# Five pairs of split-weight buffers, four raw buffers, and the layer norms' weight subtractions on VectorE

## The chip, the cores and the metric

The kernel runs on one core of a Trainium2 chip, in one launch. The metric is the device time of an execution in microseconds (us). Times of the kernel before are the median of three runs.

## The reference

The program computes two transformer blocks in float32 for one sequence of 256 tokens with 1024 features. The first block makes a modulation from a condition vector, mixes the tokens by attention, a state-space scan and a pooled branch, and passes them through 16 experts, of which each token uses two. The second block is two layers of feed-forward, token mix, feed-forward and per-layer gate, with a layer norm behind each:

```python
def second_block(x, p, ln_g, ln_b, ffn_w1, ffn_w3, ffn_w2, w_in, ...):
    a = DEEPNORM_ALPHA_2
    for i in range(DEPTH_2):
        x = _layer_norm(a * x + MACARON_W * _swiglu(x, ffn_w1[i, 0], ffn_w3[i, 0], ffn_w2[i, 0]), ln_g[i, 0], ln_b[i, 0])
        mix = token_mixing(x, w_in[i], ...)
        x = _layer_norm(a * x + mix, ln_g[i, 1], ln_b[i, 1])
        x = _layer_norm(a * x + MACARON_W * _swiglu(x, ffn_w1[i, 1], ffn_w3[i, 1], ffn_w2[i, 1]), ln_g[i, 2], ln_b[i, 2])
        ple = jax.nn.sigmoid(x @ ple_w_gate[i]) * (p[i] @ ple_w_proj[i])
        x = _layer_norm(a * x + ple, ln_g[i, 3], ln_b[i, 3])
    return x
```

The token mix has three branches: an RWKV recurrence, a gated delta rule (which inverts small triangular matrices) and a gated linear attention.

## The kernel before

Nearly all the time goes into products of the 256 tokens with weights that stream in from HBM. Each weight matrix is cut into chunks of 128 x 1024 values, 512 KB. A chunk (`chunk_ap`, L139 to L152) is loaded by SyncE's (SP's) queue into a buffer `raw`; ScalarE (ACT) casts it to `whi`, a rounded float32 that TensorE (PE) multiplies at its faster rate (L112); a subtraction raw - whi gives the rest, `wlo` (L113, which the profile shows under the helper's line L88). The activations are split in the same way into `xh` and `xl`, or `ffh` and `ffl`. PE makes three products for each block: whi with xh, whi with xl, wlo with xh, into PSUM banks `psA`, `psB`, `psC` (L85). There are five buffers `raw`, and three each of `whi` and `wlo`; a `raw` is free again when its subtraction is done, a `whi` and a `wlo` when PE has used them. The modulation's weights (`ada`, L260) pass through the same five `raw` buffers, but are multiplied and summed on VectorE (DVE) into `adacc` instead.

The subtraction runs on DVE, or on GpSimd (POOL) while the counter `s.on_pool` is above 0. The counter falls by one with each chunk and is set anew at certain places: at the start (L351), in the first mix (L370), at the end of `first_out` (L769), in `experts` (L922), at the end of `moe` (L981) and of `res_ln` (L1057), in the token mix (L1710, L1716), and ahead of the projection of the per-layer input (L1768).

A scheduler sets the order of the instructions on each engine by priorities and by when buffers come free: chunks are split 400 places ahead of the work in which they stand (`SPLIT_AHEAD`), and a layer norm goes ahead of other work by 2000 (`LN_AHEAD`). Each engine then runs its list strictly in order.

Between two stages stands a layer norm (`res_ln`, L1039, with `ln_apply`, L237). For each half of the tokens DVE adds the residual (`lnr<-psA,x`), takes the statistics (`lnst`, `lnmv`), and ACT the root (`lnrs`); DVE normalises in two halves of 512 columns (`lnr<-lnr,lnmv,lng` and `x<-lnr,lnrs,lnb`); PE transposes x into `psC` (L117), ACT and DVE split it into `xh` and `xl`. Ahead of the experts and behind them the same is written out in `first_out` (L706) and `moe` (L943, with the names `mo`). The gains and offsets `lng` and `lnb` are loaded by POOL's queue (`load_rows`, L703). The next stage's first products use the first half of the tokens while the second half is still being normalised.

```python
    def split(s, hi, lo, src, eng=None):
        s.nc.scalar.copy(hi, src)
        s.sub(lo, src, hi.bitcast(F32), eng)
```

Of the kernel before, what the change touches and what calls it, by code (L numbers as in the profile page):

```python
# [9 lines left out]
F32 = mybir.dt.float32  # L10
# [9 lines left out]
D = 1024  # L20
# [3 lines left out]
SSD_AHEAD = 100  # L24


# which tiles take turns in which slots (by lifetime), and how many slots there are
# [29 lines left out]
class Net:  # L57
# [13 lines left out]
    # ---- tiles  # L71
# [11 lines left out]
    # ---- engines  # L83
# [51 lines left out]
    # ---- dense products  # L135
# [3 lines left out]
    def chunk_ap(s, ap, nk, ncol):  # L139
        with s.tc.high_priority(SPLIT_AHEAD):  # L140
            raw = s.wp.tile([128, nk, ncol], F32, name="raw", bufs=5)
            hi = s.wp.tile([128, nk, ncol], F32R, name="whi", bufs=3)
            lo = s.wp.tile([128, nk, ncol], F32R, name="wlo", bufs=3)
            s.nc.sync.dma_start(raw, ap)
            s.split(hi, lo, raw, s.nc.gpsimd if s.on_pool > 0 else None)
# [27 lines left out]
    def cols_s(s, w, c0, x, nk=8):  # L173
        """[128, 2, 256] bank with columns c0..c0+256 of x @ w, features on partitions."""
# [5 lines left out]
    def cols_s_half(s, ps, w, cols, x, k):  # L180
        """the part of cols_s, for several blocks of columns, that takes features k*128 .. k*128+512."""
# [3 lines left out]
    def few_cols(s, w, x, out):  # L185
        """a few columns of x @ w, as rows of out [n, 256] and in a bank [128, 2, n] with tokens on partitions."""
# [13 lines left out]
    def cols_m(s, w, c0, ncol, x, *together):  # L200
        """two banks [128, ncol], tokens on partitions (K = 1024)."""
# [5 lines left out]
    def by_token(s, todo, x, *together):  # L207
        """so many chunks at a time (one in the end) do their products with the first half of the tokens before
        those with the second half."""
# [12 lines left out]
    def to_T(s, x, t, out, k0=0, n=8):  # L222
        """token block t ([128, n*128]) -> hi/lo parts with features on partitions."""
# [7 lines left out]
    # ---- layer norm over r [128, 1024] (in place scratch) -> out  # L231
    def warm(s, dep, f=AF.Sqrt):
        """has the function's table loaded once dep [128, 1] is there."""
        j = s.t([128, 1], "warm")
        s.act(j, dep, f, scale=0.0, bias=1.0)
# [23 lines left out]
    # ---- first block  # L259
    def ada(s, sections):  # L260
        """the modulation's sections as columns of s.mod; yields after every chunk of the weights."""
        nc, a = s.nc, s.a
        for i in sections:
            acc = s.t([128, 1024], "adacc")
            for k in range(8):
                raw = s.wp.tile([128, 1024], F32, name="raw", bufs=5)
# [13 lines left out]
    def ada_row(s, i, dst, **k):  # L280
        """section i as a row on every partition."""
# [7 lines left out]
    def start(s):  # L289
# [28 lines left out]
        # shift and scale, half of the features at a time  # L318
# [3 lines left out]
        def stream(h):  # L322
            acc = s.t([128, 2, 512], "adacc")
            for k in range(8):
                raw = s.wp.tile([128, 2, 512], F32, name="raw", bufs=5)
# [24 lines left out]
        for p, c in zip(first, s.first_cols):  # L350
            s.on_pool = 1  # L351
# [22 lines left out]
    def log1pexp(s, y, shape, tag):  # L374
        """y -> max(y, 0) + log1p(exp(-|y|)), in place; log1p(e) = ln(u) * e / (u - 1), u = 1 + e."""
# [21 lines left out]
    def forget(s, w, x):  # L397
        """softplus(-f) of the forget gates, softplus(dt), exp(a_log)."""
# [12 lines left out]
    def attention(s, w, x, first, qT, kT, v):  # L411
# [7 lines left out]
        for g in range(2):  # L419
# [5 lines left out]
            if g == 0:  # L425
                nlf, dt, al = s.forget(w, x)
                # negated cumulative forget gate, per key: rows [2 (hi, lo), head, key]
# [17 lines left out]
            # heads 8g + 2i + par; even and odd ones run side by side in the array's halves  # L445
# [55 lines left out]
    def ssd_in(s, w, x, dt, al):  # L501
# [29 lines left out]
        # decays  # L531
# [18 lines left out]
    def pool_zgate(s, w, x):  # L550
        """the pooled branch; and z * (1 + tanh(z / 2)) = 2 silu(z), tokens on partitions."""
# [9 lines left out]
        for g in range(4):  # L561
# [18 lines left out]
            # the mean over the window, which the first tokens do not fill, less the token itself  # L580
# [64 lines left out]
    def merge_gates(s, w, x):  # L645
        """m = (1 + tanh(g0/2)) y_att + (1 + tanh(g1/2)) y_pool; g2 kept: all twice the gate."""
# [15 lines left out]
    def ssd_out(s):  # L662
        nc, a = s.nc, s.a
        nw = s.mod[:, 48:64]
        # z holds 2 y: mean square over 512 of y is ss / 2048
# [28 lines left out]
        # merged (twice the gated sum), then w_out  # L694
# [11 lines left out]
    def first_out(s):  # L706
        """w_out, the two layer norms, and the router's input."""
# [19 lines left out]
        # the router's product with (n * sc + sh) as one with n, which sh's share precedes  # L727
# [41 lines left out]
        s.on_pool = 3  # L769
# [1020 lines left out]
```

## Time and profile before

| what | us |
|---|---|
| median of the runs shown | 2696.99 |
| all runs | 2691.86, 2696.99, 8709.61 |
| span of the profiled execution, first to last instruction | 2692.0 |
| its PE, DVE, ACT, POOL busy time | 2537.4, 1801.1, 1293.3, 286.6 |

The page gives no time of the profiled execution other than its span, which lies at the lowest of the runs. The run of 8709.61 was disturbed; the other two lie 0.2% apart. An engine's busy time is the sum of its instructions; where PE is busy all the time, nothing that another engine does less of shortens the span. The granted clock (PEclk) is the share of full speed that the throttle gave TensorE in a stretch: 1.00 is 2.4 GHz, and the lower level of 1.2 GHz is 0.5. A wait such as "PE psC L117 <- DVE x L106" is idle time of the first engine that ended when the second had done the named instruction. All times inside the program are us from the first instruction.

### The profile page before, as it was taken

How to read it: one execution, taken by the hardware profiler on the slowest of the kernel's cores; microseconds unless marked ns; L12 is line 12 of the kernel's file. 1: busy time of each engine (PE TensorE's matmuls, PEld its weight loads, DVE VectorE, ACT ScalarE, POOL GpSimd, SP SyncE). 2: the span in 40 equal slices, each digit the busy share in tenths (PEclk: the TensorE clock that was granted, in tenths of full speed). 3: DMA queues.
4: the chain of work that ended last, by engine and by line, in shares of the span. 5: the costliest groups of instructions: out<-in, count | busy, mean ns of one | idle time of the engine just before them, and what ended most of it. 6: DMA issues, size and time to landing. Idle time of an engine off the chain costs nothing.

```text
span 2692.0 us, 41847 instructions
## 1 busy us (share of the span) xinstructions
PE 2537.4 (94%) x16713; PEld 2279.5 (85%) x16713; DVE 1801.1 (67%) x2487; ACT 1293.3 (48%) x1737; POOL 286.6 (11%) x195
## 2 busy tenths in 40 slices
PE   6999999969999899999999999989999999999997
PEld 5889889958878699787888989869978889898986
DVE  6558876678888755558647765565555855776556
ACT  3445635457777554444344544444435424444443
POOL 2000240030000010013101010020001310101001
PEclk8889989979999999999989999999999998999999
DMA  8557645538888676552223456655655323355663
GB/s 257 197 182 231 197 146 171 169 125 289 293 294 283 217 208 184 174 167 78 80 81 92 146 172 183 186 175 177 184 181 153 97 61 87 83 161 171 182 188 118
DMA packets 351198, 458.87 MB, mean 170 GB/s; under 512 B 30899, under 2 KB 242577, under 8 KB 350993
## 3 DMA queue, kind: packets, MB, share of 16 engines
q1 hardware_dynamic: 347280, 445.09, 53.9%
q0 software_dynamic: 3712, 11.01, 1.3%
q8 instruction: 133, 2.18, 0.3%
q14 instruction: 73, 0.59, 0.1%
HBM read 454.14 MB, written 1.87 MB: 169 GB/s over the span
## 4 chain that ended last, share of the span: by engine, by line
PE 54%; DVE 8%; DMA 2%; issue 1%; ACT 1%; DVEq 0%; SPq 0%; ACTq 0%
PE psA L85 44%; PE psB L85 7%; PE psC L85 2%; DVE wlo L88 1%; DVE x L106 1%; DVE dg_p L88 1%; DVE lnr L106 1%; PE psC L117 1%; DMA dg_d<-dg_T 1%; DVE dg_T L1135 0%; DMA dg_o<-dg_d 0%; DVE cv L106 0%; PE psB L117 0%; DVE lnst L1052 0%; DMA dg_d<-dg_c 0%
## 5 line engine op out<-in xcount | busy, mean ns | idle before, releaser
L112 ACT CAST whi<-raw 128x1024 fp32r<-128x1024 f32 x782 | 817.2, 1046 | 887.1 <-PE psA L85 557.4
L88 DVE TENSOR_TENSOR wlo<-raw,whi 128x1024 fp32r<-128x1024 f32 (+1 forms) x721 | 889.4, 1235 | 522.8 <-ACT whi L112 517.6
L85 PE MATMUL psA<-xh,wlo 128*128 128x256 f32 x2864 | 824.3, 288 | 7.8 <-POOL wlo L88 5.2
L85 PE MATMUL psA<-xh,whi 128*128 128x256 f32 x2864 | 823.3, 287 | 6.9 <-DVE cv L106 2.8
L85 PE MATMUL psA<-xl,whi 128*128 128x256 f32 x2864 | 822.2, 287 | 1.3 <-DVE xl L88 1.3
L85 PEld LDWEIGHTS psA<-xh,wlo 128*128 128x128 f32 x2864 | 555.9, 194 | 16.1 <-POOL wlo L88 6.1
L85 PEld LDWEIGHTS psA<-xh,whi 128*128 128x128 f32 x2864 | 555.7, 194 | 15.1 <-issue 7.8
L85 PEld LDWEIGHTS psA<-xl,whi 128*128 128x128 f32 x2864 | 556.2, 194 | 6.6 <-issue 3.6
L88 POOL TENSOR_TENSOR wlo<-raw,whi 128x1024 fp32r<-128x1024 f32 x61 | 156.2, 2570 | 1635.8 <-ACT whi L112 900.7
L85 PE MATMUL psA<-whi,xl 128*128 128x512 f32 (+1 forms) x416 | 155.9, 375 | 4.8 <-DVE xl L88 4.8
L85 PE MATMUL psA<-whi,xh 128*128 128x512 f32 (+1 forms) x416 | 155.9, 376 | 2.8 <-ACT xh L112 2.8
L85 PE MATMUL psA<-wlo,xh 128*128 128x512 f32 (+1 forms) x416 | 155.8, 375 | 2.4 <-POOL wlo L88 1.4
L85 PE MATMUL psA<-whi,ffl 128*128 128x512 f32 x352 | 138.7, 394 | 0.0
L85 PE MATMUL psA<-wlo,ffh 128*128 128x512 f32 x352 | 138.6, 394 | 0.0
L85 PE MATMUL psA<-whi,ffh 128*128 128x512 f32 x352 | 138.4, 393 | 0.0
L85 PEld LDWEIGHTS psA<-whi,xl 128*128 128x128 f32 x416 | 84.2, 202 | 19.9 <-DVE xl L88 8.4
L85 PEld LDWEIGHTS psA<-whi,xh 128*128 128x128 f32 x416 | 84.6, 203 | 15.7 <-ACT xh L112 4.4
L85 PEld LDWEIGHTS psA<-wlo,xh 128*128 128x128 f32 x416 | 84.6, 203 | 14.9 <-DVE wlo L88 1.8
L85 PEld LDWEIGHTS psA<-wlo,ffh 128*128 128x128 f32 x352 | 65.9, 187 | 15.9
L85 PEld LDWEIGHTS psA<-whi,ffl 128*128 128x128 f32 x352 | 65.9, 187 | 15.8
L85 PEld LDWEIGHTS psA<-whi,ffh 128*128 128x128 f32 x352 | 65.9, 187 | 15.8
L109 ACT ACT_TABLE_LOAD x53 | 68.0, 1283 | 1.7 <-PEq L1783 0.7
(706 smaller groups left out, 3912.9 us busy)
## 6 DMA issues: line engine op xcount, KB each, us to landing
raw<-ffn_w SPq DMA_DIRECT2D x264, 512.0 KB
raw<-w_in SPq DMA_DIRECT2D x230, 512.0 KB
raw<-w_exp_gate SPq DMA_DIRECT2D x64, 512.0 KB
raw<-w_exp_up SPq DMA_DIRECT2D x64, 512.0 KB
raw<-w_exp_down SPq DMA_DIRECT2D x64, 512.0 KB
raw<-w_ada SPq DMA_DIRECT2D x48, 512.0 KB
raw<-w_branch SPq DMA_DIRECT2D x24, 512.0 KB
raw<-w_ssm_o SPq DMA_DIRECT2D x16, 512.0 KB
```

The costliest lines, as they stand in the source:

```text
L85: s.nc.tensor.matmul(out, lhsT, rhs, start=start, stop=stop, skip_group_check=True)
L88: (eng or s.nc.vector).tensor_tensor(out, a, b, op=op)
L106: (eng or s.nc.vector).scalar_tensor_tensor(out, a, sc, b, op0=op0, op1=op1)
L109: s.nc.scalar.activation(out, a, f, **k)
L112: s.nc.scalar.copy(hi, src)
L117: s.nc.tensor.transpose(out, in_, s.ident[:n, :n])
```

## The change

The numbers of buffers become constants: four `raw` and five each of `whi` and `wlo`. In memory that is, on each partition, one buffer of 4 KB less and four more. The scratch that GpSimd's transfers use for descriptors is set to 4096 bytes, where the default was 16384. Six of the nine places that set `s.on_pool` are gone; the chunks behind them are subtracted on DVE. The places in the first mix behind the scan (L370) and in the token mix (L1710, L1716) stay. Comments and docstrings are taken out, which shifts line numbers (L88 becomes L89, L106 becomes L107, L240 L241, L1052 L1048); nothing else is changed.

```diff
+RAWS, PARTS = 4, 5
...
-            raw = s.wp.tile([128, nk, ncol], F32, name="raw", bufs=5)
-            hi = s.wp.tile([128, nk, ncol], F32R, name="whi", bufs=3)
-            lo = s.wp.tile([128, nk, ncol], F32R, name="wlo", bufs=3)
+            raw = s.wp.tile([128, nk, ncol], F32, name="raw", bufs=RAWS)
+            hi = s.wp.tile([128, nk, ncol], F32R, name="whi", bufs=PARTS)
+            lo = s.wp.tile([128, nk, ncol], F32R, name="wlo", bufs=PARTS)
...
         for p, c in zip(first, s.first_cols):
-            s.on_pool = 1
             s.cols_s_half([p], a["w_in"][0], [c], x, 0)
...
             h.append(n)
-        s.on_pool = 3
...
-            if e == 16:
-                s.on_pool = 2
...
-        s.on_pool = 2
         return x
...
-        s.on_pool = 2
         return out
...
             P = s.ffn(x, i, 1)
-            s.on_pool = 2
             pj = s.ple_proj(i)
...
-    nc = bacc.Bacc("TRN2", target_bir_lowering=False, num_devices=1)
+    nc = bacc.Bacc("TRN2", target_bir_lowering=False, num_devices=1, dynamic_dma_scratch_size=4096)
```

The scheduler works with the new numbers of buffers, so the order on the engines moves too. On DVE, at the layer norm between the first feed-forward and the token mix of block 2's first layer, the order before is this (`wlo` with a number is one chunk's rest, `x_5220` the residual stream, `xl` the next stage's input; rows on statistics and parameters that lie between are left out, here and below):

```order
L88 TENSOR_TENSOR wlo_14026<-raw_14024,whi_14025 128x1024
L106 SCALAR_TENSOR_TENSOR lnr0_14109<-psA_13866,x_5220 128x512
L1052 BN_STATS lnst_14111<-lnr0_14109 128x6
L106 SCALAR_TENSOR_TENSOR lnr0_14109<-lnr0_14109,lnmv_14119,lng_14103 128x512 x2
L106 SCALAR_TENSOR_TENSOR x_5220<-lnr0_14109,lnrs_14120,lnb_14104 128x512 x2
L106 SCALAR_TENSOR_TENSOR lnr1_14110<-psA_13867,x_5220 128x512
L88 TENSOR_TENSOR wlo_14186<-raw_14184,whi_14185 128x1024
L88 TENSOR_TENSOR xl_14108<-psC_14129,xh_14107 128x4x128
L1052 BN_STATS lnst_14112<-lnr1_14110 128x6
L106 SCALAR_TENSOR_TENSOR x_5220<-lnr1_14110,lnrs_14146,lnb_14104 128x512 x2
```

On DVE at the same layer norm, the order of the changed kernel is this:

```order
L89 TENSOR_TENSOR wlo_14026<-raw_14024,whi_14025 128x1024
L89 TENSOR_TENSOR wlo_14174<-raw_14172,whi_14173 128x1024
L89 TENSOR_TENSOR wlo_14180<-raw_14178,whi_14179 128x1024
L107 SCALAR_TENSOR_TENSOR lnr0_14109<-psA_13866,x_5220 128x512
L107 SCALAR_TENSOR_TENSOR lnr0_14109<-lnr0_14109,lnmv_14119,lng_14103 128x512 x2
L89 TENSOR_TENSOR wlo_14186<-raw_14184,whi_14185 128x1024
L107 SCALAR_TENSOR_TENSOR x_5220<-lnr0_14109,lnrs_14120,lnb_14104 128x512 x2
L107 SCALAR_TENSOR_TENSOR lnr1_14110<-psA_13867,x_5220 128x512
L89 TENSOR_TENSOR xl_14108<-psC_14129,xh_14107 128x4x128
L89 TENSOR_TENSOR wlo_14228<-raw_14226,whi_14227 128x1024
L89 TENSOR_TENSOR wlo_14252<-raw_14250,whi_14251 128x1024
L107 SCALAR_TENSOR_TENSOR x_5220<-lnr1_14110,lnrs_14146,lnb_14104 128x512 x2
```

The chunks 14174 and 14180, which POOL subtracted before, stand on DVE ahead of the norm; 14186 has gone from behind x of the first half to before it, and two more chunks, 14228 and 14252, come in the second half. On DVE at the layer norm between the second feed-forward and the per-layer gate (`pl_l` is the rest of the per-layer input), the order before is this:

```order
L88 TENSOR_TENSOR wlo_19974<-raw_19972,whi_19973 128x1024
L106 SCALAR_TENSOR_TENSOR lnr0_20076<-psA_19814,x_5220 128x512
L106 SCALAR_TENSOR_TENSOR x_5220<-lnr0_20076,lnrs_20087,lnb_20071 128x512 x2
L106 SCALAR_TENSOR_TENSOR lnr1_20077<-psA_19815,x_5220 128x512
L88 TENSOR_TENSOR xl_20075<-psC_20096,xh_20074 128x4x128
L88 TENSOR_TENSOR pl_l_20022<-psC_20016,pl_h_20021 128x512
L106 SCALAR_TENSOR_TENSOR x_5220<-lnr1_20077,lnrs_20113,lnb_20071 128x512 x2
L88 TENSOR_TENSOR wlo_20152<-raw_20150,whi_20151 128x1024
```

On DVE at that norm, the order of the changed kernel is this:

```order
L89 TENSOR_TENSOR wlo_20028<-raw_20026,whi_20027 128x1024
L89 TENSOR_TENSOR wlo_20050<-raw_20048,whi_20049 128x1024
L107 SCALAR_TENSOR_TENSOR lnr0_20076<-psA_19814,x_5220 128x512
L89 TENSOR_TENSOR wlo_20140<-raw_20138,whi_20139 128x1024
L107 SCALAR_TENSOR_TENSOR x_5220<-lnr0_20076,lnrs_20087,lnb_20071 128x512 x2
L107 SCALAR_TENSOR_TENSOR lnr1_20077<-psA_19815,x_5220 128x512
L89 TENSOR_TENSOR xl_20075<-psC_20096,xh_20074 128x4x128
L89 TENSOR_TENSOR wlo_20146<-raw_20144,whi_20145 128x1024
L89 TENSOR_TENSOR wlo_20152<-raw_20150,whi_20151 128x1024
L107 SCALAR_TENSOR_TENSOR x_5220<-lnr1_20077,lnrs_20113,lnb_20071 128x512 x2
L89 TENSOR_TENSOR pl_l_20022<-psC_20016,pl_h_20021 128x512
```

Two chunks, 20028 and 20050, now come ahead of the norm, three, 20140 to 20152, inside it, and the subtraction of `pl_l` has gone behind x of the second half. PE's list has the same number of instructions in both kernels. On PE only a few groups change places: behind the norm between the token mix and the second feed-forward, a fourth chunk's products with the first half of the tokens come ahead of the second half's transposes, where three did before.

## Rows read from the trace of the kernel before

**Rows 1.** The page: the span, and the engines' busy time.
```profile
span 2692.0 us, 41847 instructions
...
PE 2537.4 (94%) x16713; PEld 2279.5 (85%) x16713; DVE 1801.1 (67%) x2487; ACT 1293.3 (48%) x1737; POOL 286.6 (11%) x195
```
**Rows 2.** Groups by line: count | busy us, mean ns | idle us before, releasers.
```profile
L88 DVE TENSOR_TENSOR wlo<-raw,whi 128x1024 fp32r<-128x1024 f32 (+1 forms) x721 | 889.4, 1235 | 522.8 <-ACT whi L112 517.6 <-issue 0.5
L112 ACT CAST whi<-raw 128x1024 fp32r<-128x1024 f32 x782 | 817.2, 1046 | 887.1 <-PE psA L85 557.4 <-issue 171.5 <-PE psB L85 69.8
L88 POOL TENSOR_TENSOR wlo<-raw,whi 128x1024 fp32r<-128x1024 f32 x61 | 156.2, 2570 | 1635.8 <-ACT whi L112 900.7 <-ACT lnrs L109 733.5 <-issue 1.5
...
L106 DVE SCALAR_TENSOR_TENSOR x<-lnr,lnrs,lnb 128x512 f32<-128x512 f32 x36 | 49.7, 1420 | 0.2
L106 DVE SCALAR_TENSOR_TENSOR lnr<-lnr,lnmv,lng 128x512 f32<-128x512 f32 x36 | 31.2, 888 | 0.0
```
**Rows 3.** DVE's timeline, feed-forward to token mix: start us, us, instruction, [idle before].
```profile
1137.28 5.56 DVE L106 SCALAR_TENSOR_TENSOR x<-lnr,lnrs,lnb 128x512 f32<-128x512 f32 x2
...
1147.96 1.41 DVE L106 SCALAR_TENSOR_TENSOR x<-lnr,lnrs,lnb 128x512 f32<-128x512 f32 x2
...
1152.56 0.69 DVE L88 TENSOR_TENSOR xl<-psC,xh 128x512 fp32r<-128x512 f32 x1 [2.58 <-ACT xh L112]
```
**Rows 4.** POOL's timeline at the same place.
```profile
1136.59 2.81 POOL L88 TENSOR_TENSOR wlo<-raw,whi 128x1024 fp32r<-128x1024 f32 x1 [176.85 <-ACT lnrs L109]
...
1139.90 2.37 POOL L88 TENSOR_TENSOR wlo<-raw,whi 128x1024 fp32r<-128x1024 f32 x1
```
**Rows 5.** Windows there: length, busy us by engine, then PEclk, DMA share, GB/s.
```profile
1136.00:1145.00 9.00, 4.54 (x21) 2.81 (x19) 8.96 (x8) 3.95 (x7) 6.17 (x4) 0.91 0.40 103
1145.00:1152.00 7.00, 6.78 (x23) 5.46 (x24) 4.98 (x17) 0.26 (x2) 0.00 (x0) 0.63 0.40 139
```
**Rows 6.** The chain of waits there: start us, us, what.
```profile
1143.43 1.13 DVE wlo L88
...
1145.22 6.25 PE psA L85 x16
...
1152.58 7.49 PE psA L85 x31
```
**Rows 7.** DVE's timeline at the router, the experts' end and two later norms.
```profile
537.55 5.46 DVE L106 SCALAR_TENSOR_TENSOR lnr<-lnr,lnmv,lng 128x512 f32<-128x512 f32 x2
...
543.65 2.12 DVE L88 TENSOR_TENSOR lnr<-lnr,x 128x512 f32<-128x512 f32 x1
...
942.80 4.58 DVE L106 SCALAR_TENSOR_TENSOR mo<-mo,lnmv,lng 128x512 f32<-128x512 f32 x2
...
1773.18 5.42 DVE L106 SCALAR_TENSOR_TENSOR x<-lnr,lnrs,lnb 128x512 f32<-128x512 f32 x2
...
1811.57 2.67 DVE L106 SCALAR_TENSOR_TENSOR lnr<-lnr,lnmv,lng 128x512 f32<-128x512 f32 x2
```
**Rows 8.** A window of the experts' stage, columns as in rows 5.
```profile
600.00:915.00 315.00, 313.72 (x1497) 253.02 (x1496) 266.19 (x276) 229.37 (x270) 0.00 (x0) 1.00 0.87 293
```
**Rows 9.** The chain of waits in the token mixes: first and last such piece.
```profile
1275.45 1.18 DVE wlo L88
...
2335.34 1.81 DVE wlo L88
```
**Rows 10.** Waits of SP's queue: us in all, times, longest.
```profile
SPq L144 <- DVE wlo L88: 1528.6, 612, 30.6
```
**Rows 11.** Waits of ACT from 600 to 915 us.
```profile
ACT whi L112 <- PE psB L85: 68.6, 121, 0.9
```
**Rows 12.** Waits over the span: the casts' wait for w_in.
```profile
ACT whi L112 <- DMA raw<-w_in: 51.8, 25, 6.5
```
**Rows 13.** Transfers: queue, kind, count, KB each, median us to landing.
```profile
lnb<-ln_b POOLq DMA_DIRECT2D x8, 512.0 KB, 5.0
```

More of the change, by code (lines that the diff above doesn't have):

```diff
@@ L265, in ada @@
             for k in range(8):
-                raw = s.wp.tile([128, 1024], F32, name="raw", bufs=5)
+                raw = s.wp.tile([128, 1024], F32, name="raw", bufs=RAWS)
                 nc.sync.dma_start(raw, a["w_ada"][0, k * 128:k * 128 + 128, i * 1024:i * 1024 + 1024])
@@ L324, in stream @@
             for k in range(8):
-                raw = s.wp.tile([128, 2, 512], F32, name="raw", bufs=5)
+                raw = s.wp.tile([128, 2, 512], F32, name="raw", bufs=RAWS)
                 src = a["w_ada"][0, k * 128:k * 128 + 128, 0:2048].rearrange("p (i c) -> p i c", i=2)
```

## The prediction

> **What bounds the kernel now.** I read the page's busy line first, then the groups by line and tile, the timelines of DVE and POOL over the layer norms, the chain of waits, the granted clock by windows, and the waits and transfers last. The busy line says TensorE: PE is busy for 2537 of 2692 us [rows 1]. So in most stretches a change on DVE or POOL is worth nothing, and what can be won is PE's idle time, and the time in which it runs at its lower clock. The idle time lies where a result of one stage passes through a layer norm before the next product can start. There the reader should lay two timelines side by side. At 1137.28 us DVE begins the two halves of x of a layer norm and takes 5.56 us [rows 3], though the same pair takes 1.41 at 1147.96. At 1136.59 and 1139.90 POOL does two weight subtractions, of 2.81 and 2.37 us [rows 4]. Each of DVE's two instructions ends when one of POOL's does. In the window 1136 to 1145 PE is busy for 4.54 of 9 us, and behind it, from 1145 to 1152, it is granted 0.63 of its full clock [rows 5]. The chain of waits passes through this: DVE's subtraction, then 16 products in 6.25 us where 31 later ones take 7.49 [rows 6].
>
> **The change part by part.**
>
> *A. No POOL subtractions at the layer norms.* 61 subtractions stand on POOL, 721 on DVE, at 2570 and 1235 ns each [rows 2]. By the order of instructions 31 of them pass to DVE; those in the token mixes stay on POOL. What DVE loses to the collisions: the 36 x-instructions take 49.7 us; at 0.705 each (1.41 for two) [rows 3] they would take 25.4, so 24.3 are lost. It falls to six layer norms with two subtractions or more beside x: about 4 us each, as at 1137.28 [rows 3] and again at 1773.18 (5.42 less 1.41) [rows 7]. The 36 lnr-instructions take 31.2 us against 36 x 0.70 = 25.2: 6.0 lost, 4.06 of them at 537.55 (5.46 less 1.40) ahead of the router and 1.27 at 1811.57 (2.67 less 1.40) [rows 2, 7]. The mo-instructions ahead of block 2 lose 4.58 less 1.40 = 3.2, and one instruction at 543.65 loses 2.12 less 0.69 = 1.43 [rows 7]. In all some 35 us, all of it on the path, since PE waits there.
>
> Against it stand the subtractions that now lie inside the layer norms on DVE. One costs the chain 1.13 us [rows 6]. The first two of each group are no burden: by the order they come ahead of the layer norm, where DVE waits for PE anyway, and two more pairs of buffers let them. Those behind them stand in front of x or in the second half. Place by place (the stall less 1.13 for each subtraction added behind the start of the norm):
> - feed-forward to token mix, twice: 4.15 - 2 x 1.13 = 1.9, and 0.7 for one of the two that falls where DVE waits for a transpose anyway (2.58 us of wait at 1152.56) [rows 3]: 2.6, twice 5.2.
> - token mix to feed-forward, twice: 4.0 - 2 x 1.13 = 1.7; a fourth chunk's 12 products now stand ahead of the transposes on PE, a fraction of them in the way: 1.5, twice 3.0.
> - feed-forward to the per-layer gate, twice: 4.0 - 3 x 1.13 = 0.6, and the pl_l subtraction goes behind x of the second half: 0.
> - gate to feed-forward, once: 1.27 - 2 x 1.13 = -1.0.
> - end of the experts: 3.2 - 2 x 1.13 = 0.9. Router: 4.06 + 1.43 - 3 x 1.13 = 2.1.
> - the start: four POOL subtractions pass to DVE, 4.5 us, which is about what the sums of the modulation lose beside them; 0.
>
> The sum is 5.2 + 3.0 + 0 - 1.0 + 0.9 + 2.1 = 10.2 us. The ends: if no added subtraction is in the way, 35; if each of them is (31 x 1.13 = 35) and also the casts ahead of them come late, -10.
>
> The Trainium skill (SBUF — State Buffer, section "Who interferes with whom") says that a DVE instruction with two SBUF inputs contends with a GpSimd instruction that reads SBUF, and that the one which issues second is blocked for the whole of the first. The rows on x agree, 5.56 us beside 2.81 and 2.37. Taken as it stands the rule prices every subtraction on POOL, not only those beside a layer norm: it is the second rival below.
>
> *B. Five pairs instead of three.* PE hardly waits for parts in the long stretches: from 600 to 915 it is busy for 313.72 of 315 us [rows 8], so there more pairs bring nothing. In the token mixes at least 23 subtractions stand on the chain, the first at 1275.45 and the last at 2335.34 [rows 9], between the steps of the inverses. The order shows them between the same steps as before. If two in each of the four stretches go ahead of their step, 8 x 1.18 = 9.4 us; if they only move, 0; if the chunks cast earlier get in front of a step, -4. I take 4, the nearer to zero since the order keeps the pattern.
>
> *C. The clock.* Behind a layer norm 16 products take 6.25 us at a lowered clock; at the 31 products' pace of 7.49 they would take 3.9 [rows 6]. 2.4 us, at some eight places: 19 us if a shorter pause keeps the clock up everywhere, 0 if it falls as before. PE still pauses for about 2 to 3 of the 4.5 us, so I take 4.
>
> *D. Four raw buffers and less scratch.* SP issues each chunk's load when a subtraction frees a buffer; it waited 612 times for one of DVE's [rows 10]. In the experts' stage the rate is 293 GB/s, 92.3 MB in 315 us, 176 chunks of 512 KB, one in 1.79 us [rows 8]. Five raw and three pairs make eight chunks between issue and use, four and five make nine, so the run-ahead grows. But the raw buffers must also turn over: four of them allow 4 x 1.79 = 7.2 us from issue to subtraction, five 8.95. What is needed: a load of the same size lands in 5.0 us [rows 13] (POOL's queue, the nearest row), cast 1.05 and subtraction 1.24 [rows 2] behind it: 7.3, at the limit. For more room speaks that the casts there waited 121 times, 68.6 us, for PE to release a pair [rows 11], so chunks lay landed. I take 0; the ends are +2 and -79 (were all 8.95 us needed, 2.24 per chunk). For the descriptor scratch I see no more than a later lnb (5.0 us of landing, loaded a stage ahead): 0, at worst -5 at one norm.
>
> *The sum:* 10.2 + 4 + 4 + 0 = 18 us off the profiled span of 2692.0, 2674. The undisturbed runs are 2692 and 2697, so the profiled execution is at the lower of them and the median 5 above. I add 2 and forecast **2676 us**.
>
> **Edits that only look like waits.** The subtractions on DVE wait for their casts; behind one that waits stand the steps of the norm, and behind these the transposes and PE. With two more pairs the cast does not wait for PE there, so I count no stall; one late load at each of nine norms, at the 2.07 us that a cast waited for w_in (51.8 us in 25 waits) [rows 12], would cost 19. It is in the lower end of A.
>
> **The rivals.**
> 1. *No net change.* The subtractions on DVE take back what the collisions cost: 31 x 1.13 = 35 us against 35. For it: DVE is in order, and rows 3 show it without a pause through both halves. Against it: a third of them lie ahead of the norm. B and C then give 0 to 4: 2690 to 2699, at 2694. Should the pairs not run ahead at all, because four raw buffers stop the stream first, the change doesn't do what it says; the time is the same.
> 2. *Much faster.* Every one of the 31 blocks DVE for its POOL time wherever it stands: 31 x (2.57 - 1.13) = 45 us: 2692 - 45 + 2 = 2649. For it: rows 3 and 4. Against it: most DVE work outside the norms is hidden by PE [rows 1]. With C in full it would reach 2630.
> 3. *Slower: the turnover of raw buffers becomes the bound in the experts' stage.* It decides from 7.2 us on. At 8.0 us a chunk takes 2.0, 176 x 0.21 = 37 us more, less the 18 of the sum: 2692 + 37 - 18 + 2 = 2713; at 8.95, 2755. For it: 7.3 against 7.2 [rows 2, 8, 13]. Against it: the casts that waited for PE [rows 11], and the stage is bound by PE.
>
> **How the numbers follow.** The forecast (2660 to 2688 by the halved ends of A to C) 0.5; no net change 0.22; much faster 0.14; slower 0.14. The range reaches down to 2646 (most of the second rival) and up to 2708 (half of the third's cases below it): 2646 to 2708, with about 0.18 left out. A measurement of this kernel can tell about 2% from no change, 54 us. Under 2643 lies a third to a half of the second rival, 0.06; over 2751 the worst of the third, 0.04; 0.90 in between.
>
> **What would show it.** In the profile of the changed kernel: the x group's mean at 0.7 us instead of 1.42 and POOL's subtractions at 30 (A); the chain's DVE subtractions in the norms, 1.13 each, and PE's busy share from 1100 to 1200 up by 2 to 3 us; subtractions on the chain in the token mixes fewer than 23 (B); 16 products behind a norm in under 6 us, with a granted clock over 0.63 (C); the window of the experts unchanged, and casts there waiting for PE, not for loads (D). The forecast is wrong if the x group is repaired and the norms are no shorter, or if casts in the experts' stage begin to wait for loads.

## The result, and the profile after

The changed kernel takes 2731.41 us (median of four runs, 2729.49 to 2733.45), the kernel before 2694.44 beside it. The ratio is 1.0131, with a 95% interval of 1.0111 to 1.0150: slower by 1.3%, and outside the range that was forecast. One run of the kernel before (8709.61) and one of e4 (4887.97) were disturbed; they count in the medians and not in the ratios. All that follows compares single profiled executions for the place of a difference, and medians for its size; runs of one kernel lie up to 29 us apart, so a few us between two profiles say nothing.

The page of the changed kernel, span and busy time, to be read against [rows 1]:

```profile
span 2727.7 us, 41827 instructions
...
PE 2561.3 (94%) x16713; PEld 2295.5 (84%) x16713; DVE 1792.3 (66%) x2516; ACT 1303.9 (48%) x1741; POOL 212.4 (8%) x166
```

The groups by line of the changed kernel, columns as in [rows 2]:

```profile
L89 DVE TENSOR_TENSOR wlo<-raw,whi 128x1024 fp32r<-128x1024 f32 x750 | 924.4, 1234 | 548.0 <-ACT whi L113 544.6
...
L89 POOL TENSOR_TENSOR wlo<-raw,whi 128x1024 fp32r<-128x1024 f32 x32 | 79.2, 2478 | 222.3 <-ACT whi L113 222.3
...
L107 DVE SCALAR_TENSOR_TENSOR lnr<-lnr,lnmv,lng 128x512 f32<-128x512 f32 x36 | 25.8, 742 | 0.0
L107 DVE SCALAR_TENSOR_TENSOR x<-lnr,lnrs,lnb 128x512 f32<-128x512 f32 x36 | 25.5, 748 | 0.1
```

So the change did at the norms what was foreseen: x fell from 49.7 to 25.5 us and lnr from 31.2 to 25.8. DVE even lost work in all, though it does 29 more subtractions. Everything on it but the weight subtractions fell from 1801.1 - 889.4 = 911.7 to 1792.3 - 924.4 = 867.9 us: 44 us less for the same work, 29.6 of them at x and lnr. The 29 added subtractions take 35 of the 44, so DVE is busy for 9 us less in all.

DVE's timeline of the changed kernel at the norm between the first feed-forward and the token mix, to be read against [rows 3]:

```profile
1185.29 1.21 DVE L89 TENSOR_TENSOR wlo<-raw,whi 128x1024 fp32r<-128x1024 f32 x1
1186.41 1.41 DVE L107 SCALAR_TENSOR_TENSOR x<-lnr,lnrs,lnb 128x512 f32<-128x512 f32 x2
...
1194.24 1.42 DVE L107 SCALAR_TENSOR_TENSOR x<-lnr,lnrs,lnb 128x512 f32<-128x512 f32 x2
```

The windows there, columns as in [rows 5]:

```profile
1179.00:1188.00 9.00, 8.05 (x38) 6.12 (x37) 7.00 (x12) 3.48 (x6) 1.10 (x2) 1.00 0.50 149
1188.00:1195.00 7.00, 6.57 (x28) 4.71 (x28) 6.86 (x13) 1.68 (x4) 0.00 (x0) 1.00 0.53 156
```

From the first x to the second it is 7.8 us where it was 10.7 [rows 3], PE is busy for 8.05 of 9 us where it was 4.54, and the granted clock stays at 1.00, the upper level, behind the norm, where it fell to 0.63 [rows 5]. (The two windows begin at different places of the norm; as far into it as the one of before, from 1184 to 1193, PE is busy for 8.05 us as well.) At this place the forecast was too careful, if anything. Yet the program is longer. The question is where, and two tiles tell it: x of the layer norms, and yl, which ends each expert's last product. First the kernel before (count: minimum/median/maximum ns, first and last start in us):

```profile
L106 DVE SCALAR_TENSOR_TENSOR x<-lnr,lnrs,lnb x36: 735/747/2962, 546.4 to 2688.0; 128x512 f32<-128x512 f32 x36
...
L106 DVE SCALAR_TENSOR_TENSOR x<-mo,lnrs,lnb x4: 739/742/745, 938.4 to 949.8; 128x512 f32<-128x512 f32 x4
...
L106 DVE SCALAR_TENSOR_TENSOR yl<-psB,ws,yh x32: 730/744/747, 615.0 to 929.8; 128x512 fp32r<-128x512 f32 x32
```

The same tiles in the changed kernel:

```profile
L107 DVE SCALAR_TENSOR_TENSOR x<-lnr,lnrs,lnb x36: 741/748/754, 570.9 to 2723.6; 128x512 f32<-128x512 f32 x36
...
L107 DVE SCALAR_TENSOR_TENSOR x<-mo,lnrs,lnb x4: 747/748/748, 984.8 to 994.8; 128x512 f32<-128x512 f32 x4
...
L107 DVE SCALAR_TENSOR_TENSOR yl<-psB,ws,yh x32: 736/746/752, 641.9 to 976.3; 128x512 fp32r<-128x512 f32 x32
```

The first layer norm, behind the first mix, comes to its x 24.5 us later. The experts, from the first yl to the last, take 334.4 instead of 314.8 us: 19.6 more. Block 1, to the start of its last x, ends 45.0 us later. From there to the end of the span it is 1732.9 instead of 1742.2: block 2 won 9.3. The loss is all in the two stages of block 1 that are not layer norms.

What PE and ACT wait for in the experts' stage is this in the kernel before (us in all, times, longest; from 615 to 930 us):

```profile
ACT whi L112 <- DMA raw<-w_exp_down: 11.1, 15, 1.6
...
ACT whi L112 <- DMA raw<-w_exp_gate: 1.6, 4, 0.8
...
PE psA L85 <- ACT yh L109: 2.9, 3, 1.4
```

and the window, columns as in [rows 5]:

```profile
615.00:930.00 315.00, 310.45 (x1469) 248.90 (x1468) 262.67 (x275) 224.77 (x264) 5.70 (x2) 1.00 0.83 281
```

In the changed kernel, from 642 to 976 us:

```profile
ACT whi L113 <- DMA raw<-w_exp_down: 22.9, 25, 1.9
...
ACT whi L113 <- DMA raw<-w_exp_up: 10.3, 9, 1.8
...
ACT whi L113 <- DMA raw<-w_exp_gate: 8.4, 13, 1.1
...
PE psA L86 <- ACT yh L110: 17.0, 21, 2.4
```

with the window:

```profile
642.00:976.00 334.00, 315.82 (x1469) 250.68 (x1467) 261.56 (x273) 225.15 (x262) 0.00 (x0) 0.99 0.81 264
```

The casts wait 41.6 us for loads instead of 12.7. ACT is in order, so yh stands behind a cast that waits, and PE, which needs yh, waits with it: 17.0 us instead of 2.9. The rate falls from 281 to 264 GB/s although the transfers have room (DMA share 0.81). A stage that takes fewer bytes a second and waits for them seems to have too few loads on the way; the experiments test it. In the first mix it is the same (waits of ACT, before from 60 to 300 us):

```profile
ACT whi L112 <- DMA raw<-w_in: 31.5, 21, 2.9
...
ACT whi L112 <- DMA raw<-w_attn_o: 3.7, 2, 2.6
```

and in the changed kernel, from 60 to 325 us:

```profile
ACT whi L113 <- DMA raw<-w_in: 45.0, 28, 3.6
...
ACT whi L113 <- DMA raw<-w_attn_o: 11.4, 6, 3.2
```

### The profile page after: what moved, and what is told of

Its sections match the earlier page's. It is cut to its first block, busy times and chain, and to the rows that moved or that the text cites. A ratio compares the mean times of both kernels' runs of the same rounds, so it can differ in the third digit from the quotient of the medians.

```text
span 2727.7 us, 41827 instructions
## 1 busy us (share of the span) xinstructions
PE 2561.3 (94%) x16713; PEld 2295.5 (84%) x16713; DVE 1792.3 (66%) x2516; ACT 1303.9 (48%) x1741; POOL 212.4 (8%) x166
## 4 chain that ended last, share of the span: by engine, by line
PE 54%; DVE 6%; ACT 2%; DMA 1%; issue 1%; DVEq 0%; ACTq 0%; SPq 0%
PE psA L86 44%; PE psB L86 7%; PE psC L86 2%; DVE wlo L89 1%; PE psC L118 1%; DVE lnr L107 1%; DMA raw<-ffn_w 1%; ACT whi L113 0%; DVE x L107 0%; DMA dg_o<-dg_d 0%; DVE xl L89 0%; PE psB L118 0%; DMA dg_d<-dg_T 0%; DVE gl_M L89 0%; DVE lnst L1048 0%
## 5 line engine op out<-in xcount | busy, mean ns | idle before, releaser
L89 DVE TENSOR_TENSOR wlo<-raw,whi 128x1024 fp32r<-128x1024 f32 x750 | 924.4, 1234 | 548.0 <-ACT whi L113 544.6
L86 PEld LDWEIGHTS psA<-xh,whi 128*128 128x128 f32 x2864 | 561.9, 196 | 15.0 <-issue 5.7
L89 POOL TENSOR_TENSOR wlo<-raw,whi 128x1024 fp32r<-128x1024 f32 x32 | 79.2, 2478 | 222.3 <-ACT whi L113 222.3
```

The costliest lines, as they stand in the source:

```text
L86: s.nc.tensor.matmul(out, lhsT, rhs, start=start, stop=stop, skip_group_check=True)
L89: (eng or s.nc.vector).tensor_tensor(out, a, b, op=op)
```

## The experiments

Three theories stood at the start. R: four raw buffers turn over too slowly, which costs block 1. P: the casts and subtractions of the fourth and fifth pair stand in front of other work and wait there. S: the subtractions that pass from POOL to DVE cost it. The table gives all runs: raw buffers and pairs; where POOL's subtractions at the start, the router, the experts and the norms are kept; the median; the ratio to the kernel before on the same chip with its interval; and from the one profile of each the start of block 1's last x, the time from first to last yl, and the span left for block 2.

| run | raw, pairs | POOL kept | median us | ratio, 95% | block 1 ends | experts | block 2 |
|---|---|---|---|---|---|---|---|
| before | 5, 3 | all | 2694.44 | 1 | 949.8 | 314.8 | 1742.2 |
| changed | 4, 5 | none | 2731.41 | 1.0131 [1.0111, 1.0150] | 994.8 | 334.4 | 1732.9 |
| e1 | 4, 3 | all | 2723.59 | 1.0117 [1.0100, 1.0134] | 976.5 | 330.2 | 1746.7 |
| e2 | 4, 5 | all | 2716.28 | 1.0100 [1.0081, 1.0120] | 989.1 | 332.4 | 1722.7 |
| e3 | 5, 3 | none | 2688.11 | 0.9979 [0.9964, 0.9994] | 943.8 | 316.1 | 1742.3 |
| e4 | 5, 4 | none | 2682.34 | 0.9956 [0.9931, 0.9982] | 946.1 | 315.9 | 1744.3 |
| e5 | 4, 3 | none | 2725.37 | 1.0107 [1.0059, 1.0156] | 973.4 | 329.7 | 1751.9 |
| e6 | 5, 4 | all | 2677.68 | 0.9947 [0.9920, 0.9974] | 947.8 | 317.0 | 1732.5 |
| e7 | 5, 4 | block 2 | 2679.02 | 0.9961 [0.9943, 0.9978] | 941.4 | 317.6 | 1733.0 |
| e8 | 6, 4 | block 2 | 2669.32 | 0.9915 [0.9882, 0.9948] | 934.5 | 312.0 | 1726.4 |
| e9 | 5, 3, scratch 4096 | all | 2691.27 | 0.9993 [0.9975, 1.0011] | 953.3 | 318.7 | 1743.2 |
| e10 | 4, 5 | block 2 | 2722.86 | 1.0115 [1.0094, 1.0136] | 992.5 | 331.4 | 1725.7 |
| e11 | 8, 3 | block 2 | 2680.76 | 0.9959 [0.9944, 0.9975] | 938.7 | 312.5 | 1741.4 |
| e12 | 4 + 2, 4 | block 2 | 2734.39 | 1.0150 [1.0131, 1.0169] | 1001.6 | 332.8 | 1741.6 |
| e13 | 4, 5, pl_l early | none | 2705.47 | 1.0040 [1.0020, 1.0060] | 994.9 | 334.0 | 1708.2 |
| e14 | 6, 4, pl_l early | none | 2655.14 | 0.9871 [0.9839, 0.9902] | 928.9 | 312.4 | 1719.6 |

**e1, only four raw buffers.** In the kernel before:

```diff
-            raw = s.wp.tile([128, nk, ncol], F32, name="raw", bufs=5)
+            raw = s.wp.tile([128, nk, ncol], F32, name="raw", bufs=4)
```

(and the same at the two loads of the modulation).

> The kernel before with four raw buffers in place of five; three pairs, POOL's subtractions and the scratch as before. In the changed kernel the last x of the experts' end starts at 994.8 us where it was 949.8 before, and the rest takes 1728.8 where it was 1738.2: block 1 lost some 45 us, block 2 won 9. Theory R (four raw buffers turn over too slowly): the whole loss of block 1 is here, so about 2692 + 45 = 2737 us, at least 2725, and nothing of the 9 is won. Theory P (casts and subtractions of a fourth and fifth pair stand in front of other work and wait there for loads): 2692, within 8. Theory S (the subtractions that pass from POOL to DVE cost more there): 2692, within 8.

The one number gives 31 us of loss, and 15.4 of them in the experts' stage:

```profile
L106 DVE SCALAR_TENSOR_TENSOR yl<-psB,ws,yh x32: 735/746/752, 626.8 to 957.0; 128x512 fp32r<-128x512 f32 x32
```

R holds for this, P and S do not explain it. But it is less than the 2725 that R asked for at least, and of block 1's 45 us only 26.7 are here, so something else adds to the changed kernel's loss.

**e2, four and five with POOL kept.** In the kernel before: raw 4, `whi` and `wlo` 5, the scratch at 4096; the nine settings of `s.on_pool` stay.

> The kernel before with four raw buffers, five pairs and the smaller scratch, but with all of POOL's subtractions kept. Theory R: as slow in block 1 as the changed kernel (end of the experts at 985 to 1000 us) and without the 9 us won at the later norms, 2730 to 2745. Theory P: the same, 2730 to 2745. Theory S: block 1 as before, 2692 within 8.

24 us slower, not 38 to 50 as R and P said: block 2 took 1722.7 us, the shortest of the table up to here. The pairs win 24 us in block 2 against e1, and lose 12.6 in block 1, which is a part for P. The changed kernel, which differs by POOL's subtractions alone, is slower than e2 by 15 us in the medians and by some 8 in the ratios, whose intervals overlap a little. So R is most of the story, but S seems to have a part, and not where S put it.

**e3, only POOL's subtractions taken out.** In the changed kernel:

```diff
-RAWS, PARTS = 4, 5
+RAWS, PARTS = 5, 3
```

> The changed kernel with five raw buffers and three pairs: of the change only the removal of POOL's subtractions at the norms (and the smaller scratch) is left. Theory R: block 1 as before, the experts' end at 945 to 955 us, and what the norms win, 2680 to 2692. Theory P: the same. Theory S: block 1 slow, over 2715.

As R said: 0.9979, some 6 us. The gain is all in block 1 (943.8), none of it in block 2 (1742.3).

**e4, five raw buffers and four pairs.** `RAWS, PARTS = 5, 4` in the changed kernel.

> The changed kernel with five raw buffers and four pairs, which still fit. Theory R: no loss in block 1 (experts' end at 940 to 955 us) and the norms' gain as in the changed kernel: 2675 to 2690. Theory P: half of the loss, since one more pair of the two is there: 2700 to 2715. Theory S: as the changed kernel, 2725 to 2735.

0.9956: the loss is gone with one raw buffer more, though a pair of P's is still there. R. In its one profile block 2 is as long as before; its other runs lie between 2664.64 and 2693.46, and the profiled one, with a span of 2690.4, is among the long ones.

**e5, four raw buffers, three pairs, no POOL.** `RAWS, PARTS = 4, 3` in the changed kernel.

> The changed kernel with three pairs again (four raw buffers, none of POOL's subtractions at the norms). Theory R as it stands now: four raw buffers cost 31 us with POOL's subtractions and three pairs; without those at the norms every subtraction waits its turn on DVE, a raw buffer is held longer, and the loss grows: 2731 or more, with block 1's end over 985 us. If the parts simply add up: 2723.6 - 4.5 = 2719, block 1's end at 971. Theory P (it is the deeper pairs that make the changed kernel slower than the one with POOL kept): 2719 or less.

Between the two cases, with a wide interval; block 1's end at 973.4 is what the parts give when added. That DVE holds the raw buffers longer without POOL, and so makes the loss grow, is not borne out. The row of x sets the pairs' price beside four raw buffers:

```profile
L107 DVE SCALAR_TENSOR_TENSOR x<-lnr,lnrs,lnb x36: 733/745/748, 553.9 to 2721.3; 128x512 f32<-128x512 f32 x36
```

The first x comes at 553.9 us here and at 570.9 in the changed kernel, which differs by its two more pairs alone. They lengthen block 1 by 21.4 us, 17.0 of them ahead of this x, and shorten block 2 by 19.0. Beside five raw buffers a fourth pair does no such harm: from e9 to e6 block 1 is 5.5 us shorter, from e3 to e4 2.3 longer. So a quarter to a half of block 1's 45 us (12.6 by e1 and e2, 21.4 here) comes from the deeper pairs, and only together with four raw buffers.

**e6, five raw buffers, four pairs, POOL kept; e7, POOL only in block 2.** e6 is the kernel before with `whi` and `wlo` at 4 and the scratch at 4096; e7 is that with three settings of `s.on_pool` less:

```diff
-            s.on_pool = 1
...
-        s.on_pool = 3
...
-            if e == 16:
-                s.on_pool = 2
```

> The kernel before with four pairs in place of three, five raw buffers, POOL's subtractions kept, smaller scratch. In block 2 the kernel with POOL kept took 1723 us with five pairs and 1747 with three, the one without POOL at the norms 1729 with five and 1742 with three. Theory R with DVE as the price of the norms: POOL at block 2's norms is worth some 10 us once the pairs run ahead, so block 2 in 1727 to 1735, in all 2675 to 2685. If the removal of POOL's subtractions is what won the 9 us in block 2: 1738 or more there, and 2690 or more in all.

> Five raw buffers, four pairs, smaller scratch; POOL's subtractions taken out at the start, ahead of the router and in the experts, and kept at the norms of block 2. Without them block 1 ended 6.0 us earlier at five raw buffers. Theory R with DVE as the price: both gains, block 1's end at 941 to 946 us, block 2 in 1727 to 1735, in all 2668 to 2680. If POOL at the norms of block 2 is worth nothing: as with all of them taken out, 2682.

Both are inside what was expected. Both beat the kernel before; neither can be told from the other or from e4.

**e8, six raw buffers; e11, eight and three pairs.** e7 with `bufs=6` for raw, and with `bufs=8` and three pairs: the same memory as the changed kernel, spent on loads.

> As the run before it, with six raw buffers. Theory R: if five still turn over too slowly in block 1, a sixth wins a part of what the fifth did (27 us in block 1): 5 to 15 us there, 2660 to 2670 in all. If five are enough: the same within 4 us.

> The memory of the changed kernel spent the other way: eight raw buffers, three pairs, POOL's subtractions kept at block 2's norms only. Theory R: block 1 as good as with six raw buffers or better, its end at 925 to 936 us; block 2 as with three pairs, 1736 to 1743 us, since there the pairs are what counts: 2662 to 2680 in all. If raw buffers past five bring nothing: block 1's end at 944, 2685 in all.

e8 wins 0.85%. Its waits of ACT in the experts' stage, from 603 to 915 us, are these two and no others:

```profile
ACT whi L112 <- PE psB L85: 78.4, 145, 0.8
ACT yh L109 <- PE psB L85: 7.8, 2, 5.0
```

No cast waits for a load any more. The expert rows of six and eight raw buffers agree (yl, first e8 and then e11), so beyond six there is nothing to win in that stage, and 312 us is about what PE itself needs (it is busy for 308.59 of them):

```profile
L106 DVE SCALAR_TENSOR_TENSOR yl<-psB,ws,yh x32: 732/745/750, 603.0 to 915.0; 128x512 fp32r<-128x512 f32 x32
```

```profile
L106 DVE SCALAR_TENSOR_TENSOR yl<-psB,ws,yh x32: 732/744/747, 605.8 to 918.3; 128x512 fp32r<-128x512 f32 x32
```

e11's block 1 was expected at 925 to 936 and came to 938.7, which made it 2680.76 where 2662 to 2680 was expected; its block 2, with three pairs, is as long as before. So the raw buffers are worth their memory in block 1, and the pairs in block 2.

**e9, only the smaller scratch.** In the kernel before, `dynamic_dma_scratch_size=4096`.

> The kernel before with the descriptor scratch at 4096 bytes and nothing else changed. If the scratch is free, as priced: 2691 within 5 us. If the smaller scratch holds up POOL's transfers and with them lnb or the inverses' data: over 2700, with longer landings on POOL's queue.

0.9993, and lnb lands after 4.8 us as a median where it was 5.0 [rows 13]: free, as priced.

**e10, the changed kernel with POOL kept at block 2's norms.** e7 with `bufs=4` and `bufs=5`.

> Four raw buffers and five pairs as in the changed kernel, POOL's subtractions taken out of block 1 and kept at block 2's norms. With POOL kept everywhere this took 2716 (experts' end at 989, block 2 in 1723 us), with POOL removed everywhere 2731 (995 and 1733). If the 15 us between them are the two places added up: block 1 ends at 993 to 997, block 2 takes 1719 to 1727, in all 2717 to 2724. If what block 1 loses without POOL is only scatter of that one profile: its end at 989, 2712 to 2717.

Block 2 at 1725.7 is near e2's 1722.7, and block 1 at 992.5 lies between e2's 989.1 and the changed kernel's 994.8. By the medians the two places add up, with some 8 us of the 15 in block 2; by the ratios this kernel is clear neither of e2 nor of the changed one.

**e12, four raw buffers for the weights and two for the modulation.** e8 with

```diff
-                raw = s.wp.tile([128, 1024], F32, name="raw", bufs=6)
+                raw = s.wp.tile([128, 1024], F32, name="raw_ada", bufs=2)
```

at both loads of the modulation, and raw at 4 for the weights.

> As the run with six raw buffers and four pairs, but with the six divided: four for the weight chunks and two of their own for the modulation's weights, which are streamed during the first mix. Theory R: during the first mix the weights have four to themselves, so the mix loses little (the router's products done by 551 to 560 us where six gave 551 and the changed kernel 590), but the experts' stage, where no modulation is loaded, runs on four: 17 to 20 us longer than with six (312 us between the first and last yl), 2680 to 2692 in all. If the loss in the first mix is not from sharing the raw buffers but from the weights' own count: router at 570 or later, over 2695.

A miss in the whole: 2734, with the first x at 577.5 us. By the letter of the expectation that would speak for the weights' own count. But two buffers for the modulation starve the start, where DVE waits for them from the first (waits of DVE, 0 to 80 us):

```profile
DVE adacc L106 <- DMA raw_ada<-w_ada: 13.8, 8, 4.6
```

Behind that start lies the same work of PE, some 1660 products, in e12, in the kernel before and in the changed kernel, in this order (columns as in [rows 5]):

```profile
80.00:335.00 255.00, 243.17 (x1659) 221.73 (x1659) 169.94 (x246) 120.37 (x221) 17.14 (x28) 0.92 0.58 185
...
51.00:303.00 252.00, 243.60 (x1664) 219.46 (x1665) 176.01 (x253) 124.40 (x228) 14.71 (x27) 0.93 0.65 206
...
55.00:329.00 274.00, 249.87 (x1662) 224.98 (x1662) 182.33 (x254) 125.56 (x228) 20.54 (x29) 0.90 0.62 192
```

It takes 255 us, about as long as with five shared buffers, where four shared ones take 274. So past the start, four buffers that the weights have to themselves do nearly as well as five that they share. This points to the sharing, but e12 comes to this stretch with five or six weight chunks more already loaded, so it is no clean test.

The second part came as expected. From 649.2 to 982.0 the experts take 332.8 us, 20.8 more than e8 with the same memory:

```profile
L106 DVE SCALAR_TENSOR_TENSOR yl<-psB,ws,yh x32: 732/745/749, 649.2 to 982.0; 128x512 fp32r<-128x512 f32 x32
```

So in all seven kernels with four raw buffers, e13 included, it takes 329.7 to 334.4 us, in those with five 314.8 to 318.7, with six or eight 312.0 to 312.5, whatever the pairs and POOL do. That is R, shown for the experts. How the loss in the first mix divides between the weights' own count, the sharing and the deeper pairs stays open.

**e13, the changed kernel with pl_l early.** What was left of S: why does block 2 lose when POOL's subtractions go? PE's timeline of the changed kernel ahead of the per-layer gate has a pause (start, us, instruction, [idle before]):

```profile
1819.39 2.29 PE L118 MATMUL psC<-ident,x 128*128 128x128 f32 x8 [4.49 <-DVE x L107]
1821.33 0.78 PE L86 MATMUL psA<-whi,pl_l 128*128 128x512 f32 x1
```

PE waits for x of the second half, with products of the per-layer input in its list behind it that need pl_l, which the order had put behind that same x. The edit gives the split the norms' priority:

```diff
-        s.split(pT[0], pT[1], q)
+        with s.tc.high_priority(LN_AHEAD):
+            s.split(pT[0], pT[1], q)
```

> The changed kernel with one thing added: the split of the per-layer input (pl_h, pl_l) has the layer norms' priority, so that pl_l stands on DVE behind x of the norm's first half and no longer behind x of its second. In the changed kernel PE stood idle for 4.49 us there (at 1819.39) with the products of pl_l behind it, and from the x ahead of the gate to the x behind it went 40.3 us and 36.5 us in the two layers, where the kernel with POOL kept took 35.1 and 30.8. If that move of pl_l is what the removal of POOL's subtractions costs in block 2: 35 to 37 and 31 to 33, in all 2720 to 2726, and no wait of over 3 us for x on PE there. If it is DVE's subtractions inside the norm: 40 and 36 again, 2729 to 2733.

26 us less than the changed kernel, more than expected. The x rows of the norm ahead of the gate and of the one behind it, in the changed kernel, second halves:

```profile
1818.49 1.41 DVE L107 SCALAR_TENSOR_TENSOR x<-lnr,lnrs,lnb 128x512 f32<-128x512 f32 x2
...
1858.79 1.41 DVE L107 SCALAR_TENSOR_TENSOR x<-lnr,lnrs,lnb 128x512 f32<-128x512 f32 x2
...
2686.52 1.42 DVE L107 SCALAR_TENSOR_TENSOR x<-lnr,lnrs,lnb 128x512 f32<-128x512 f32 x2
...
2722.98 1.41 DVE L107 SCALAR_TENSOR_TENSOR x<-lnr,lnrs,lnb 128x512 f32<-128x512 f32 x2
```

and in e13:

```profile
1819.36 1.41 DVE L107 SCALAR_TENSOR_TENSOR x<-lnr,lnrs,lnb 128x512 f32<-128x512 f32 x2
...
1851.15 1.41 DVE L107 SCALAR_TENSOR_TENSOR x<-lnr,lnrs,lnb 128x512 f32<-128x512 f32 x2
...
2669.98 1.41 DVE L107 SCALAR_TENSOR_TENSOR x<-lnr,lnrs,lnb 128x512 f32<-128x512 f32 x2
...
2698.36 1.42 DVE L107 SCALAR_TENSOR_TENSOR x<-lnr,lnrs,lnb 128x512 f32<-128x512 f32 x2
```

40.3 and 36.5 us became 31.8 and 28.4: 16.6 of the 26 us in these two stretches, and less than the 35.1 and 30.8 of e2. Counted from the first lnr of the norm ahead, so that the shorter norm counts too, the two places take 52.3 and 48.4 us in the changed kernel, 50.0 and 45.2 in e2, 44.5 and 41.1 in e13. So the pause was the place of pl_l, not the subtractions: with these in the norm and pl_l early, both places are shorter than with POOL kept. The late pl_l stands in e3, e4 and e5 as well: from x to x they and the changed kernel take 39.5 to 40.3 and 35.5 to 37.0 us, all kernels with POOL kept 35.1 to 38.6 and 30.8 to 34.0. The other 9 us are not explained: in that one profile layer 2's token mix was some 8 us shorter too, and nothing in the edit reaches it.

**e14, six raw buffers, four pairs, no POOL, pl_l early.**

```diff
-RAWS, PARTS = 4, 5
+RAWS, PARTS = 6, 4
```

on top of e13.

> Six raw buffers, four pairs, none of POOL's subtractions at the norms, and the early pl_l. With POOL kept at block 2's norms six and four took 2669. If pl_l was the price of taking POOL out: as good or better, 2655 to 2670. If DVE's subtractions inside the norms are a price of their own: 2675 to 2685.

2655.14 us, 0.9871 of the kernel before: at the low end of what was expected, and faster than both kernels. Whether taking out POOL's subtractions pays, with raw buffers enough and pl_l in its place, is not shown by this alone: e8, with POOL kept in block 2, has its pl_l in the old place, the two intervals overlap, and no run has the early pl_l with POOL kept.

## Why the prediction was wrong

*What bounds the kernel.* Right for long stretches with the five raw buffers, but read too firmly: "a change on DVE or POOL is worth nothing" there holds only as long as the loads keep up, and PE's 313.72 of 315 us [rows 8] did not show how near they were to not doing so. The program lost 37 us where 18 were to be won: block 1 lost 45, block 2 won 9.

*A, the norms.* The mechanism was right: x and lnr at their undisturbed time, subtractions of 1.13 us in the chain, a norm shorter by 1.8 us (13.6 to 11.8 from lnr to the end of x, by the two timelines). 29 subtractions passed to DVE, where I had read 31. The term was 10 us. Alone, in e3, it was 6 us, and it lay at the start and in the first mix, where I had put 0, with block 2 unchanged: that it came near the term is luck. With five pairs and four raw buffers it was -15 by the medians, -8 by the ratios (e2 to the changed kernel). The step that failed here is a line of the sum: the pl_l subtraction "goes behind x of the second half: 0". I had seen the move in the order and asked only what it costs DVE. PE's products that need pl_l fill its pause in the norm; moved behind x, they leave it empty for 4.49 us. e13 shows 16.6 us for the two places, and 15.0 counted from the start of the norms. Since pl_l is late in e3 too, it ate there a part of what the norms of block 2 had won.

*B and C, pairs and clock.* Too small. I took 4 and 4. Two more pairs win 24 us in block 2 from e1 to e2, and 19 from e5 to the changed kernel, which is nearer to the upper ends, 9.4 + 19; no run divides this between the pairs and the clock, whose mean over the span is 0.952 in the changed kernel and 0.955 before. In the changed kernel the clock stays at 1.00 behind the norm to the token mix, where I thought that PE's remaining pause would bring it down as before: PE had its products of the second half to do, and paused for 1 us of 9, not 2 to 3. Against it the pairs cost 12.6 us (e1 to e2) to 21.4 us (e5 to the changed kernel) in block 1 beside four raw buffers, which I had not priced. Why was not shown by a run of its own.

*D, the raw buffers.* This is the step that failed and decided the result. I put the need of a raw buffer at 7.3 us and the room at 4 x 1.79 = 7.2, called that "at the limit", and took 0, because casts had waited for PE. The room was right and the need was a little too small. Between first and last yl PE does the products of 173 chunks (1036 products, six a chunk). With six raw buffers that is 312.0 / 173 = 1.80 us a chunk, PE's own pace, so four buffers have 7.2 us. In the changed kernel it is 334.4 / 173 = 1.93 us, at which four buffers turn over in 7.7; from the issue of a load to the end of its subtraction, paired in order, the median in its trace is 7.5 us, where I had 7.3. Over 7.2 the buffers set the pace, and the stage took 19.6 us more where the term was 0. I had written that it decides from 7.2 us on, and had named the sign, casts in this stage that begin to wait for loads: they waited 41.6 us instead of 12.7. The 121 waits for PE were 0.57 us each, while one raw buffer less takes 1.8 us of room: that cover was too thin by its own row [rows 11], and a cast that waits for PE in one place says nothing of the 15 that waited for loads already. In the first mix I did not price four buffers at all, although the modulation's loads take turns in the same buffers and casts of w_in already waited 25 times for 2.07 us [rows 12]. That was the larger part: 24.5 us to the first norm, of which e1 shows 10 for the raw buffers alone, and e2 and e5 another 7 to 17 for the deeper pairs beside them.

*The scratch.* Free, as forecast.

*The rivals.* The third was the right mechanism in one of the two stages, at 2713 for its middle and 2755 for its end; its 0.14 was too little for a step that my own numbers put past the limit. That the measured time lies between the two is partly luck: at its middle it priced 37 us for the experts, who lost 19.6, and it had nothing for the first mix, which lost 24.5. The other two fell. "No net change" was wrong since parts of 10 to 30 us of both signs add up. "Much faster" counted every POOL subtraction, 45 us net; DVE's busy time fell by 9 us net, and off the path that gave PE nothing. The Trainium skill (SBUF — State Buffer, "Who interferes with whom") has the one that issues second blocked for the whole instruction. The x rows agree, with 5.56 us beside POOL's 2.81 and 2.37 and 1.41 alone. Taken for each of the 29 the rule would give 29 x 2.57 = 75 us of DVE's time, and the groups show 44.

## What to carry to other kernels

When a change trades buffers between two steps of one pipeline, price the turnover of the one that loses: its room is its count times the pace of the engine that bounds the stage, its need is load plus every step until release, and where the two are within a few per cent, the buffer that goes is the bound. Waits of a cast for its load, already in the trace of before, are the sign to look for, in every stage and not only in the one that looks critical. Of an instruction that a scheduler moves, ask what the bounding engine has queued behind it: one small subtraction in the wrong place cost more here (16.6 us at two norms) than taking 29 large ones off POOL won in all while it stood there (6 us, e3).

## What was not expected of the hardware

The clock behind a short pause: with PE busy for 8.05 of 9 us across the norm the granted clock stayed at 1.00, and with 4.54 of 9 it went to 0.63 in the next 7 us; 16 products took 6.25 us there, where the pace of the 31 later ones gives 3.9, so some 2.4 us at this place went with the pause. And transfer engines with time to spare were no help to a stage short of buffers: at 264 GB/s, with 0.81 of the engines' time, it waited, while with six raw buffers the same loads went at 280 GB/s, with 0.83, and no cast waited for one.
